# Moving modulation vectors from the attention stage into the first down projection, and splitting activations once

## The chip, the cores and the metric

The kernel runs on one core of a Trainium2 chip. The metric is the device time of one execution in microseconds; a time is the median of several runs.

## The reference

One transformer-like block on 512 tokens of width 1024, batch 1, all in float32. A condition vector c gives nine modulation vectors of 1024 numbers: shift, scale and gate of each of three sublayers.

```python
c_act = silu(c)
ada = c_act @ w_ada + b_ada          # w_ada: 1024 x 9216
sh1, sc1, g1, sh2, sc2, g2, sh3, sc3, g3 = split(ada, 9)
h = rmsnorm(x, ffn1_norm) * (1 + sc1) + sh1
x = x + 0.5 * g1 * (silu(h @ wg) * (h @ wu)) @ w_out1      # 1024 -> 2816 -> 1024
h = rmsnorm(x, mix_norm) * (1 + sc2) + sh2
z = h @ w_in        # latents, chunk q, k, v, two branch gates
y_a = latent_attention(z) @ w_branch_a
y_b = chunk_attention(z, rel_bias) @ w_branch_b
x = x + g2 * ((sigmoid(gA) * y_a + sigmoid(gB) * y_b) @ w_out)
h = rmsnorm(x, ffn2_norm) * (1 + sc3) + sh3
x = x + 0.5 * g3 * (silu(h @ wg2) * (h @ wu2)) @ w_out2
return rmsnorm(x, final_norm)
```

## The kernel before

**Number format.** Each float32 operand of a matmul is split into a high part (a cast by ACT, `L199`) and a low part (source minus high part, by DVE or POOL, `L200`). A product is three matmuls: high by high, low by high, high by low (`mm3`, L212; its three lines L215, L216 and L217 are the names by which the profile shows them).

**Stages** in order of time, in us of the profiled execution: a first piece of the up projection with the first two modulation vectors (0 to 55), the rest of the first up projection (to 252, `up_plain` and `up_fast`), the first `down` (252 to 378), the attention stage called the mixer (to about 700), a `down` with w_out (to 756), the second up projection (to 995) and the second `down` (to 1120).

**`down` (L637).** Two halves of 512 output columns. A half runs over 11 steps u; a step loads a 512 KB weight tile (`raw<-w2a`), splits it (`wh`, `wl`), splits the activations of two blocks of 128 features (`act_h`, `act_l`, `act_parts` at L632) and does 24 matmuls of 512 columns into four PSUM banks, one per block of 128 tokens. Half 1 holds back its last three steps and does them token block by token block, so that the update of x (L669, L670), the norm and the transposes (L253) of a block can begin while the next block is multiplied.

**Modulation vectors** (`vectors`, L345) are a generator. Vectors are numbered 0 to 8 (shift, scale and gate of the three sublayers). One step of it is one 512 KB load of w_ada and one DVE instruction: for shift and scale a row dot product (`ada_dot`, L301), for a gate a multiply-add into a row (`ada_step`, L297). After the eighth step of a gate its row is split and summed over partitions by four matmuls with a matrix of ones (`ada_rows`, L320; L327 and L328), and ACT writes it out (L329). Before the change vector 2 runs in `up_fast`; 4 and 3 in the first `down`, one step per u (16 loads); 7, 6 and 5 in the mixer, one step each time the helper `Fill` begins a projection (its `side`, L142), and what is left after the attention; 8 in the second `down`.

**The mixer** alternates heads of attention (`Head`, L67) with projections that `Fill` (L122) puts between. A head computes scores (L215 to L217 or L990, L991 on PE), a mask and row minimum (L83 on DVE), an exponential (L85 on ACT), a reciprocal and a scaling (L86, L87 on DVE), transposes (L95 on PE), a split of these (L98 on ACT, L99 on DVE) and the product with the values (L109 on PE). Weights are split by ACT and POOL there.

**Order and buffers.** PE's order is the order of the code. The order of the other engines is set by the framework's scheduler, which works from its own estimate of when inputs are ready. Every weight of these stages passes through one ring `raw` of 4 tiles of 512 KB, loaded in order by SP (`raw`, L192); the split weights through a ring `wh`/`wl` of 3 pairs; activations and other things through 22 tiles of one size (`slot`). ACT's own queue loads x again for the first `down` (L1053).

Of the kernel before, what the change touches and what calls it, by code (L numbers as in the profile page):

```python
# [10 lines left out]
F32 = mybir.dt.float32  # L11
F32R = mybir.dt.float32r
# [6 lines left out]
P = 128  # L19
S = 512  # L20
D = 1024
# [3 lines left out]
NF = FF // P  # L25
# [15 lines left out]
LAG_DOWN, LAG_OUT = 2, 0  # L41
EARLY_UP, FLUSH_UP = 3, (0, 2)
F1, F2 = 2, 2
WEIGHTS_A = ("raw",) * 4 + ("ada",)
WEIGHTS_B = ("raw",) * 4 + ("gate",) * 2 + ("ada",)
FLUSH_LAT = {0: 2, 1: 1}
# [20 lines left out]
class Head:  # L67
    def __init__(self, blk, h, scores, mask, v, out):
        self.blk, self.nc, self.h, self.scores_into, self.mask, self.out = blk, blk.nc, h, scores, mask, out
        self.probs = blk.sc4((P, 10 * P))  # L70
        self.st = blk.stat()
        self.v = v
        self.offs = [P * (qi * (qi + 1) // 2) for qi in range(NT)]
        self.pts = {}
# [45 lines left out]


class Fill:  # L122
    def __init__(self, ahead, side):
        self.jobs, self.ready, self.run, self.ahead, self.side = [], [], None, ahead, side

    def add(self, prepare, run):
        self.jobs.append((prepare, run))
# [6 lines left out]
    def __call__(self, n):  # L134
        while n > 0:
            if self.run is None:
                self.look(1)
                if not self.ready:
                    return
                run, units = self.ready.pop(0)  # L140
                self.run = run(units)
                self.side()  # L142
                self.look(self.ahead)
            try:
                next(self.run)
                n -= 1
            except StopIteration:
                self.run = None
# [5 lines left out]
class Block:  # L154
# [149 lines left out]
    def ada_columns(self, vec):  # L304
        io, nc = self.io, self.nc
        layer, kind = divmod(vec, 3)
        res = self.ring.tile([P, KT], F32, tag="adac", name="adac", bufs=2) if kind else self.shift[layer]
        for m in range(KT):
            self.ada_dot(self.raw(D, io["w_ada"][vec, m]), vec, m, res[:, m:m + 1])
            yield m == KT - 1  # L310
        if kind:
            col = (COL_FFN1, COL_MIX, COL_FFN2)[layer]
            nc.vector.scalar_tensor_tensor(
                self.scale[layer], res, 1.0, self.cols[:, col:col + KT], op0=ALU.add, op1=ALU.mult)
        yield True
# [1 line left out]
    def gate_row(self, name="gate_bc"):  # L317
        return self.fix.tile([P, D], F32, tag="gate", name=name, bufs=2)

    def ada_rows(self, acc):  # L320
        nc = self.nc
        hi, lo = (self.ring.tile([P, D], F32R, tag="w" + p, name="gate_" + p) for p in "hl")
        self.split(acc, hi, lo)
        for hf in range(2):
            cs = slice(hf * 512, (hf + 1) * 512)
            ps = self.bank(self.ada_bank)
            nc.tensor.matmul(ps, self.ones, hi[:, cs], start=True, stop=False)  # L327
            nc.tensor.matmul(ps, self.ones, lo[:, cs], start=False, stop=True)  # L328
            nc.scalar.mul(acc[:, cs], ps, 0.5)  # L329

    def ada_gate(self, vec):
        io, nc = self.io, self.nc
        layer = vec // 3
        if layer not in self.gate:
            self.gate[layer] = self.gate_row()
        acc = self.gate[layer]
        nc.gpsimd.memset(acc, 0.0)
        nc.scalar.dma_start(acc[0:1], io["b_ada"][:, vec * D:(vec + 1) * D])
        for j in range(KT):
            self.ada_step(acc, j, self.raw(D, io["w_ada"][vec, j]))  # L340
            yield j == KT - 1
        self.ada_rows(acc)
        yield True

    def vectors(self, vecs):  # L345
# [284 lines left out]
                side(n)  # L630

    def act_parts(self, u):  # L632
        pair = [self.slot([P, 2, S], F32R, "act_" + p) for p in "hl"]
        self.split(self.acts[u], *pair)
        return [[z[:, j] for z in pair] for j in range(2)]

    def down(self, parts, nk, w2, layer, tail, after, lag=0, store=None, side=None):  # L637
        nc = self.nc
        nu = nk // 2
# [256 lines left out]

    def mix(self, after):
        nc = self.nc
        gen = self.vectors((7, 6, 5))
        self.fill = Fill(2, lambda: self.advance(gen, 1))  # L900
        merged = self.attention()
        for _ in range(3):
            self.advance(gen, 99)
        self.low_engine = nc.vector
        self.x = self.fix.tile([P, NT, D], F32, tag="x16", name="x_back")
        for t in range(NT):
            nc.scalar.dma_start(self.x[:, t], self.x_home[t])

        parts = lambda u: [[merged[2 * u + j][:, i] for i in range(2)] for j in range(2)]
        self.down(parts, KT, self.io["w_out"], 1, KT // 2, after, LAG_OUT, store=self.slot)  # L910
# [130 lines left out]

    def layer(self, banks):
        nc, io = self.nc, self.io
        self.acts = []
        for f in range(F0):
            self.swiglu(f, banks[2 * f], banks[2 * f + 1])
        self.rope_angles()
        self.up_plain(io["w1a"], range(F0, F0 + F1), {0: self.mix_all})
        gen = self.vectors((2,))
        self.up_fast(io["w1a"], range(F0 + F1, NF), WEIGHTS_A, lambda n: self.advance(gen, n > 4))  # L1050
        self.x = self.fix.tile([P, NT, D], F32, tag="x16", name="x_again")
        for t in range(NT):
            nc.scalar.dma_start(self.x[:, t], io["x"][t * P:(t + 1) * P])  # L1053
        late = self.vectors((4, 3))
        self.down(self.act_parts, NF, io["w2a"], 0, 3, lambda t, xn: self.norm_token(t, 1, xn), LAG_DOWN,
                  side=lambda hf, u: self.advance(late, 1))
        self.mix(lambda t, xn: self.norm_token(t, 2, xn))

        def finish(t, o32):
            z = self.slot([P, D], F32, "out")  # L1060
            nc.gpsimd.tensor_tensor(z[:, :512], self.x[:, t, :512], fin[:, :512], op=ALU.mult)
            nc.vector.tensor_tensor(z[:, 512:], self.x[:, t, 512:], fin[:, 512:], op=ALU.mult)
            nc.scalar.mul(z[:, :512], z[:, :512], self.rstd[:, t:t + 1])
            nc.sync.dma_start(io["out"][t * P:(t + 1) * P, :512], z[:, :512])
            nc.vector.tensor_scalar(z[:, 512:], z[:, 512:], self.rstd[:, t:t + 1], None, op0=ALU.mult)
            nc.scalar.dma_start(io["out"][t * P:(t + 1) * P, 512:], z[:, 512:])
        gen = self.vectors((8,))
        self.acts = []
        for t in range(NT):
            nc.scalar.dma_start(self.x_home[t], self.x[:, t])  # L1070
        mixes = {EARLY_UP + j - 1: lambda j=j: self.mix_tokens(j) for j in range(2)}
        self.up_plain(io["w1b"], range(F2), mixes, EARLY_UP, FLUSH_UP)
        self.up_fast(io["w1b"], range(F2, NF), WEIGHTS_B)
        fin = self.gate_row("final_gain")
        nc.scalar.dma_start(fin, io["final"].to_broadcast([P, D]))
        self.x = self.fix.tile([P, NT, D], F32, tag="x16", name="x_last")
        for t in range(NT):
            nc.scalar.dma_start(self.x[:, t], self.x_home[t])
        self.ada_bank = "mm"

        def side(hf, u):
            if not hf:
                self.advance(gen, 1 if u < 9 else 99)
        self.down(self.act_parts, NF, io["w2b"], 2, 3, finish, side=side)
# [79 lines left out]
```

## Time and profile before

| what | us |
|---|---|
| median of 3 runs (lowest, highest) | 1136.0 (1134.95, 1137.53) |
| the profiled execution's own time | 1129.48 |
| its span in the trace | 1127.7 |
| PE busy in the span | 1074.9 |
| DVE busy in the span | 806.4 |
| ACT busy in the span | 589.4 |
| POOL busy in the span | 140.1 |

The span is what the trace shows from the first to the last instruction; the own time is that of the same execution. PE = TensorE matmul, PEld = its weight load, DVE = VectorE, ACT = ScalarE, POOL = GpSimd, SP = SyncE, which here only issues loads. A row of the timeline gives start, duration, engine, line, operation, the tiles written and read, and in brackets the idle time before it and what ended that. Tiles of one name are many buffers.

### The profile page before, as it was taken

To read this page: it belongs to the slowest core of one execution; us is meant where nothing else is said; L and a number is where in the kernel's file an instruction comes from. 1 tells how busy PE (TensorE), PEld (TensorE's weight loads), DVE (VectorE), ACT (ScalarE), POOL (GpSimd) and SP (SyncE) were. 2 spreads that over 40 slices of the span, in tenths; PEclk is the share of its full clock that TensorE was granted. 3 is DMA by queue.
4 is the path that set the end of the run, shared out by engine and by line. 5 is a ranking of instruction groups with operands and counts; after the bars stand their busy time and mean duration, and the time that the engine had idled before them with its cause. 6 is when DMAs were issued, how large, how long until landed. Compare 5 with 4: busy or idle time off the path is not lost.

```text
span 1127.7 us, 16891 instructions
## 1 busy us (share of the span) xinstructions
PE 1074.9 (95%) x6496; PEld 944.1 (84%) x6496; DVE 806.4 (72%) x1297; ACT 589.4 (52%) x1086; POOL 140.1 (12%) x126
## 2 busy tenths in 40 slices
PE   4999999999999999999889799999999999999997
PEld 3789999988887879877777678888999999988885
DVE  5898899877774767776877831458978788676724
ACT  5545555654443757655556533337555555654512
POOL 1000000000000112333443335200000000000200
PEclk9999999999999999999999999999999999999999
DMA  9723445257554422323443322442333333274322
GB/s 361 254 94 107 139 156 163 94 203 222 170 170 146 162 80 76 131 94 112 127 130 127 122 91 79 151 166 94 114 107 99 112 113 112 77 256 136 108 61 75
DMA packets 43575, 152.04 MB, mean 135 GB/s; under 512 B 5219, under 2 KB 5219, under 8 KB 43494
## 3 DMA queue, kind: packets, MB, share of 16 engines
q1 hardware_dynamic: 38160, 136.20, 36.6%
q10 hardware_dynamic: 5334, 14.76, 3.5%
q8 instruction: 51, 0.84, 0.3%
q14 instruction: 30, 0.25, 0.1%
HBM read 144.65 MB, written 6.29 MB: 134 GB/s over the span
## 4 chain that ended last, share of the span: by engine, by line
PE 76%; DVE 9%; DMA 5%; ACT 5%; issue 2%; POOL 2%; ACTq 0%; POOLq 0%; DVEq 0%
PE ps_mm L215 7%; PE ps_mm L216 7%; PE ps_mm L217 7%; PE ps_s L578 5%; PE ps_s L576 5%; PE ps_s L577 5%; DMA raw<-w_ada 3%; PE ps_t L578 3%; PE ps_t L577 3%; PE ps_t L576 3%; PE ps_s L216 2%; PE ps_s L217 2%; PE ps_s L215 2%; PE ps_t L215 2%; PE ps_t L216 2%
## 5 line engine op out<-in xcount | busy, mean ns | idle before, releaser
L199 ACT CAST wh<-raw 128x1024 fp32r<-128x1024 f32 x148 | 155.1, 1051 | 158.3 <-PE ps_o L217 47.7
L200 DVE TENSOR_TENSOR wl<-raw,wh 128x1024 fp32r<-128x1024 f32 x116 | 142.4, 1230 | 67.6 <-ACT wh L199 67.4
L215 PE MATMUL ps_mm<-h_hi,wh 128*128 128x512 f32 (+1 forms) x264 | 103.3, 391 | 0.0
L217 PE MATMUL ps_mm<-h_hi,wl 128*128 128x512 f32 (+1 forms) x264 | 100.5, 381 | 1.9 <-DVE wl L200 1.9
L216 PE MATMUL ps_mm<-h_lo,wh 128*128 128x512 f32 (+1 forms) x264 | 100.5, 381 | 0.2 <-DVE h_lo L200 0.2
L200 POOL TENSOR_TENSOR wl<-raw,wh 128x1024 fp32r<-128x1024 f32 x32 | 77.6, 2428 | 84.9 <-ACT wh L199 84.8
L578 PE MATMUL ps_s<-sum_h,wl 128*128 128x256 f32 x296 | 82.8, 280 | 0.0
L578 PE MATMUL ps_t<-sum_h,wl 128*128 128x256 f32 x296 | 82.7, 279 | 0.0
L577 PE MATMUL ps_t<-sum_l,wh 128*128 128x256 f32 x296 | 82.7, 279 | 0.0
L576 PE MATMUL ps_t<-sum_h,wh 128*128 128x256 f32 x296 | 82.6, 279 | 0.0
L577 PE MATMUL ps_s<-sum_l,wh 128*128 128x256 f32 x296 | 82.6, 279 | 0.0
L576 PE MATMUL ps_s<-sum_h,wh 128*128 128x256 f32 x296 | 82.6, 279 | 0.0
L200 DVE TENSOR_TENSOR act_l<-act,act_h 128x1024 fp32r<-128x1024 f32 x44 | 53.2, 1221 | 23.8 <-PE ps_t L216 20.2
L222 POOL TENSOR_TENSOR rstd<-ss,neghalf 128x1 f32<-128x1 f32 x16 | 10.4, 648 | 468.2 <-DVE ss L232 459.3
L217 PEld LDWEIGHTS ps_mm<-h_hi,wl 128*128 128x128 f32 x264 | 50.7, 192 | 12.3 <-DVE wl L200 2.1
L85 ACT ACTIVATE sc<-sc,stat 128x128 f32<-128x128 f32 (+1 forms) x64 | 35.9, 561 | 45.9 <-DVE stat L83 45.5
L216 PEld LDWEIGHTS ps_mm<-h_lo,wh 128*128 128x128 f32 x264 | 50.9, 193 | 7.5 <-DVE h_lo L200 0.4
L215 PEld LDWEIGHTS ps_mm<-h_hi,wh 128*128 128x128 f32 x264 | 51.0, 193 | 7.1
L578 PEld LDWEIGHTS ps_s<-sum_h,wl 128*128 128x128 f32 x296 | 55.6, 188 | 0.1
L301 DVE CUSTOM_DVE_ANT_0 raw<-raw,c_row,cols_sb 128x1024 f32<-128x1024 f32 x32 | 41.0, 1281 | 20.6 <-DMA raw<-w_ada 18.3
L576 PEld LDWEIGHTS ps_t<-sum_h,wh 128*128 128x128 f32 x296 | 55.7, 188 | 0.0
L577 PEld LDWEIGHTS ps_t<-sum_l,wh 128*128 128x128 f32 x296 | 55.6, 188 | 0.0
(380 smaller groups left out, 3289.2 us busy)
## 6 DMA issues: line engine op xcount, KB each, us to landing
raw<-w_ada SPq DMA_DIRECT2D x56, 512.0 KB, 3.6
raw<-w1a SPq DMA_DIRECT2D x32, 512.0 KB, 3.5
raw<-w1b SPq DMA_DIRECT2D x28, 512.0 KB, 3.5
raw<-w2a SPq DMA_DIRECT2D x22, 512.0 KB, 3.7
raw<-w2b SPq DMA_DIRECT2D x22, 512.0 KB, 3.7
w_first<-w_first SPq DMA_DIRECT2D x16, 512.0 KB, 9.6
raw<-w_gate SPq DMA_DIRECT2D x16, 512.0 KB, 3.5
raw_g<-w1b SPq DMA_DIRECT2D x11, 512.0 KB, 3.6
```

The costliest lines, as they stand in the source:

```text
L85: nc.scalar.activation(p, p, AF.Exp, scale=-1.0, bias=low, accum_out=tot)
L199: nc.scalar.copy(hi, src)
L200: (low_engine or nc.vector).tensor_tensor(lo, src, hi.bitcast(F32), op=ALU.subtract)
L215: mm(ps, lh, rh, start=start, stop=False)
L216: mm(ps, lh, rl, start=False, stop=False)
L217: mm(ps, ll, rh, start=False, stop=stop)
L222: nc.gpsimd.tensor_tensor(out, mean, self.neghalf[:, :n], op=ALU.pow)
L301: self.nc.vector.tensor_tensor_reduce(w, w, self.c_row, 1.0, self.cols[:, b:b + 1], ALU.mult, ALU.add, out)
L576: mm(ps, hi[:, cs], lh, start=start and k == 0, stop=False, skip_group_check=not start)
L577: mm(ps, hi[:, cs], ll, start=False, stop=False, skip_group_check=not start)
L578: mm(ps, lo[:, cs], lh, start=False, stop=k == 3, skip_group_check=not start)
```

## The change

Vectors 7, 6 and 5 (24 loads, 16 dots and 8 multiply-adds, and the four matmuls of gate 5) go from the mixer into the first `down`. There two steps per u run for the vectors 4, 3, 7, 6 and 5 (only one half-1 step, u = 10, has none), and the three steps that are left, the last of which makes the gate's row, stand behind `down`. `Fill` loses its `side`. The gate is summed up in another tile (`ada_acc`, in the place "ada"), and its row is allocated when it is made.

Activations are split once instead of in each half: `act_parts` keeps the pairs of u = 3 to 6 in the tiles hH and hL (the normed tokens, whose last reader is `up_fast`), those of u = 1, 2 and 7 to 10 in slots, and puts u = 0's pair of half 0 into the `wh`/`wl` ring; u = 0 alone is split again in half 1. That holds for both large `down` stages. Lines from L632 on stand 12 to 15 lower in the changed kernel.

```diff
@@ class Fill
-    def __init__(self, ahead, side):
-        self.jobs, self.ready, self.run, self.ahead, self.side = [], [], None, ahead, side
+    def __init__(self, ahead):
+        self.jobs, self.ready, self.run, self.ahead = [], [], None, ahead
...
                 self.run = run(units)
-                self.side()
                 self.look(self.ahead)
@@ class Block
-    def ada_rows(self, acc):
+    def ada_rows(self, acc, out):
...
-            nc.scalar.mul(acc[:, cs], ps, 0.5)
+            nc.scalar.mul(out[:, cs], ps, 0.5)
 
     def ada_gate(self, vec):
         io, nc = self.io, self.nc
         layer = vec // 3
-        if layer not in self.gate:
-            self.gate[layer] = self.gate_row()
-        acc = self.gate[layer]
+        acc = self.gate[layer] if layer in self.gate else self.main.tile([P, D], F32, tag="ada", name="ada_acc", bufs=1)
...
-        self.ada_rows(acc)
+        if layer not in self.gate:
+            self.gate[layer] = self.gate_row()
+        self.ada_rows(acc, self.gate[layer])
         yield True
...
     def act_parts(self, u):
-        pair = [self.slot([P, 2, S], F32R, "act_" + p) for p in "hl"]
-        self.split(self.acts[u], *pair)
+        if u not in self.act_pairs:
+            if not u and u not in self.act_seen:
+                pair = [self.ring.tile([P, 2, S], F32R, tag="w" + p, name="act_" + p) for p in "hl"]
+            else:
+                if u in ACT_IN_H:
+                    o = 2 * (u - ACT_IN_H[0])
+                    pair = [z[:, o:o + 2] for z in (self.hH, self.hL)]
+                else:
+                    pair = [self.slot([P, 2, S], F32R, "act_" + p) for p in "hl"]
+                self.act_pairs[u] = pair
+            self.split(self.acts[u], *pair)
+            self.act_seen.append(u)
+        else:
+            pair = self.act_pairs[u]
         return [[z[:, j] for z in pair] for j in range(2)]
...
     def mix(self, after):
         nc = self.nc
-        gen = self.vectors((7, 6, 5))
-        self.fill = Fill(2, lambda: self.advance(gen, 1))
+        self.fill = Fill(2)
         merged = self.attention()
-        for _ in range(3):
-            self.advance(gen, 99)
...
-        late = self.vectors((4, 3))
-        self.down(self.act_parts, NF, io["w2a"], 0, 3, lambda t, xn: self.norm_token(t, 1, xn), LAG_DOWN,
-                  side=lambda hf, u: self.advance(late, 1))
+        late = self.vectors((4, 3, 7, 6, 5))
+
+        def vector_steps(hf, u):
+            for _ in range(2):
+                if hf < 1 or u < 10:
+                    self.advance(late, 1)
+        self.down(self.act_parts, NF, io["w2a"], 0, 3, lambda t, xn: self.norm_token(t, 1, xn), LAG_DOWN, side=vector_steps)
+        for _ in range(8):
+            self.advance(late, 1)
         self.mix(lambda t, xn: self.norm_token(t, 2, xn))
```

**Where instructions move: the start of the first `down`, DVE.** L621 and L628 end the last step of `up_fast`. The row L301 that reads raw_2838 is the fourth dot of the late vectors in the changed kernel; raw_2760, wh_2762 and wl_2763 are the weight of u = 0. Before:

```order
L301 ISA raw_2869,adac_2794<-raw_2869,c_row_99,cols_sb_78 128x1024
L301 ISA adac_2794 128x1
L619 TENSOR_TENSOR sc4_2656<-ps_t_2653,sc4_2656 128x256
L621 TENSOR_TENSOR sc4_2656<-ps_s_2652,sc4_2656 128x256
L628 TENSOR_TENSOR act_2628<-sc4_2656,sc4_2747 128x2x2x128
L200 TENSOR_TENSOR wl_2763<-raw_2760,wh_2762 128x1024
L200 TENSOR_TENSOR wl_2801<-raw_2798,wh_2800 128x1024
```

In the changed kernel a dot more stands between L619 and L621, another between L628 and the low part of the first weight, and the low part of u = 0's activations, which stood further ahead, stands behind that:

```order
L619 TENSOR_TENSOR sc4_2656<-ps_t_2653,sc4_2656 128x256
L301 ISA raw_2838,adac_2794<-raw_2838,c_row_99,cols_sb_78 128x1024
L301 ISA adac_2794 128x1
L621 TENSOR_TENSOR sc4_2656<-ps_s_2652,sc4_2656 128x256
L628 TENSOR_TENSOR act_2628<-sc4_2656,sc4_2747 128x2x2x128
L301 ISA raw_2875,adac_2794<-raw_2875,c_row_99,cols_sb_78 128x1024
L301 ISA adac_2794 128x1
L200 TENSOR_TENSOR wl_2763<-raw_2760,wh_2762 128x1024
L200 TENSOR_TENSOR act_l_2767<-act_461,act_h_2766 128x1024
L200 TENSOR_TENSOR wl_2804<-raw_2801,wh_2803 128x1024
```

**SP at the same place.** The loads of the changed kernel, of which raw_2875 is the eighth from u = 0's weight on:

```order
L194 DMA raw_2760<-w2a 128x1024
L194 DMA raw_2795<-w_ada 128x1024
L194 DMA raw_2798<-w_ada 128x1024
L194 DMA raw_2801<-w2a 128x1024
L194 DMA raw_2835<-w_ada 128x1024
L194 DMA raw_2838<-w_ada 128x1024
L194 DMA raw_2841<-w2a 128x1024
L194 DMA raw_2875<-w_ada 128x1024
L194 DMA raw_2878<-w_ada 128x1024
L194 DMA raw_2881<-w2a 128x1024
```

Before, loads of w2a and of w_ada took turns one by one; now two of w_ada follow each of w2a.

**The end of the first `down`, PE.** In the changed kernel the four matmuls of gate 5 stand between the last matmul of `down` (L217, ps_o) and the first of the mixer (L215, wlat):

```order
L216 MATMUL ps_o<-wl,act_h 128x512
L217 MATMUL ps_o<-wh,act_l 128x512
L327 MATMUL ps_t<-gate_h,ones 128x512
L328 MATMUL ps_t<-gate_l,ones 128x512
L327 MATMUL ps_t<-gate_h,ones 128x512
L328 MATMUL ps_t<-gate_l,ones 128x512
L215 MATMUL ps_s<-wlat,h_hi 128x416
```

On DVE, gate_l stands behind the update of x for the last token block (there L681 and L682, which were L669 and L670):

```order
L681 TENSOR_TENSOR sc_3669<-ps_o,gate_bc 128x512
L200 TENSOR_TENSOR h_lo<-sc_3573,h_hi 128x4x128
L682 TENSOR_TENSOR x_again<-x_again,sc_3669 128x512
L200 TENSOR_TENSOR gate_l<-ada_acc,gate_h 128x1024
```

Before, these four matmuls and this split stood between two projections in the mixer.

## Rows read from the trace of the kernel before

**Rows 1.** Windows, first down and mixer: busy (count) of PE, PEld, DVE, ACT, POOL; PEclk, DMA share, GB/s.
```profile
252.00:374.00 122.00, 121.24 (x522) 97.10 (x523) 83.31 (x103) 52.21 (x67) 1.09 (x2) 1.00 0.59 189
400.00:655.00 255.00, 231.59 (x1245) 193.72 (x1244) 188.95 (x474) 148.24 (x355) 84.65 (x77) 0.97 0.33 108
```

**Rows 2.** Costliest groups by form, DVE, 400 to 655: busy, mean ns | idle before, releaser.
```profile
L301 DVE CUSTOM_DVE_ANT_0 raw<-raw,c_row,cols_sb 128x1024 f32<-128x1024 f32 x14 | 17.9, 1281 | 14.0 <-DMA raw<-w_ada 11.8 <-issue 2.0
L297 DVE SCALAR_TENSOR_TENSOR gate_bc<-raw,cact,gate_bc 128x1024 f32<-128x1024 f32 x8 | 12.4, 1556 | 6.4 <-DMA raw<-w_ada 6.2
```

**Rows 3.** Waits of PE, 400 to 655: total us, times, longest.
```profile
PE ps_o L109 <- DVE pt L99: 9.1, 9, 2.4
PE ps_t L95 <- DVE sc L87: 6.7, 3, 2.9
PE ps_s L990 <- DVE stat L83: 3.9, 3, 2.1
```

**Rows 4.** The same waits of PE, 400 to 500.
```profile
PE ps_o L109 <- DVE pt L99: 3.7, 5, 1.8
```

**Rows 5.** Timeline of the mixer at two vector steps, DVE and PE.
```profile
517.87 1.28 DVE L301 CUSTOM_DVE_ANT_0 raw<-raw,c_row,cols_sb 128x1024 f32<-128x1024 f32 x1 [3.19 <-DMA raw<-w_ada]
...
520.54 0.33 PE L95 MATMUL ps_t<-ident,sc 128*128 128x128 f32 x1 [2.08 <-DVE sc L87]
...
583.73 3.46 DVE L297 SCALAR_TENSOR_TENSOR gate_bc<-raw,cact,gate_bc 128x1024 f32<-128x1024 f32 x1 [2.37 <-DMA raw<-w_ada]
...
587.64 0.38 PE L109 MATMUL ps_o<-pt,vs 128*128 128x256 f32 x1 [2.43 <-DVE pt L99]
```

**Rows 6.** Timeline of the mixer at a weight split on POOL.
```profile
466.27 4.73 POOL L200 TENSOR_TENSOR wl<-raw,wh 128x1024 fp32r<-128x1024 f32 x2 [4.56 <-ACT wh L199]
...
468.61 2.61 DVE L87 TENSOR_SCALAR sc<-sc,stat 128x384 f32<-128x384 f32 x1
```

**Rows 7.** Windows of the mixer at a lower granted clock.
```profile
521.90:525.30 3.40, 3.40 (x12) 2.92 (x11) 2.40 (x10) 2.16 (x7) 2.13 (x1) 0.50 0.24 52
590.20:593.60 3.40, 3.40 (x10) 2.65 (x9) 2.27 (x3) 0.59 (x2) 0.63 (x2) 0.51 0.66 263
644.80:651.60 6.80, 6.01 (x18) 4.87 (x17) 3.86 (x14) 2.68 (x9) 0.00 (x0) 0.50 0.22 78
```

**Rows 8.** Timeline, 672 to 680: gate 5's row.
```profile
675.58 1.23 DVE L200 TENSOR_TENSOR gate_l<-gate_bc,gate_h 128x1024 fp32r<-128x1024 f32 x1 [0.90 <-ACT gate_h L199]
675.60 0.50 PE L327 MATMUL ps_t<-gate_h,ones 128*128 128x512 f32 x1 [0.95 <-ACT gate_h L199]
676.86 0.50 PE L328 MATMUL ps_t<-gate_l,ones 128*128 128x512 f32 x1 [0.76 <-DVE gate_l L200]
```

**Rows 9.** Timeline at the start of the first down.
```profile
247.75 1.28 DVE L301 CUSTOM_DVE_ANT_0 raw<-raw,c_row,cols_sb 128x1024 f32<-128x1024 f32 x1 [0.96 <-DMA raw<-w_ada]
...
249.07 0.33 SPq L194 DMA_DIRECT2D raw<-w2a  x1
...
253.46 0.40 PE L217 MATMUL ps_s<-wh,act_l 128*128 128x512 f32 x1
```

**Rows 10.** Tile raw, 240 to 262: its DMA.
```profile
DMA to landing us min/median/max: 3.6/4.4/7.0
```

**Rows 11.** Window at the start of the first down.
```profile
249.00:254.00 5.00, 2.84 (x18) 2.18 (x17) 3.55 (x7) 3.89 (x6) 0.00 (x0) 1.00 0.90 346
```

**Rows 12.** Costliest groups, 252 to 374: ACT's cast of weights.
```profile
L199 ACT CAST wh<-raw 128x1024 fp32r<-128x1024 f32 x21 | 22.0, 1052 | 39.9 <-PE ps_t L217 23.3 <-PE ps_o L217 16.6
```

**Rows 13.** Timeline at the end of the first down.
```profile
378.72 0.35 PE L215 MATMUL ps_s<-wlat,h_hi 128*128 128x416 f32 x1
...
380.63 0.69 DVE L670 TENSOR_TENSOR x_again<-x_again,sc 128x512 f32<-128x512 f32 x1
```

**Rows 14.** Timeline at the start of the second down.
```profile
994.97 0.38 ACT L625 ACTIVATE sc<-ps_o 128x256 f32<-128x256 f32 x1
...
996.50 0.40 PE L217 MATMUL ps_s<-wh,act_l 128*128 128x512 f32 x1
```

More of the change, by code (lines that the diff above doesn't have):

```diff
@@ L43 @@
 F1, F2 = 2, 2
+ACT_IN_H = range(3, 7)
 WEIGHTS_A = ("raw",) * 4 + ("ada",)
@@ L1043, in layer @@
         nc, io = self.nc, self.io
-        self.acts = []
+        self.acts, self.act_pairs, self.act_seen = [], {}, []
         for f in range(F0):
@@ L1067, in layer @@
         gen = self.vectors((8,))
-        self.acts = []
+        self.acts, self.act_pairs, self.act_seen = [], {}, []
         for t in range(NT):
```

## The prediction

> **What bounds the kernel now.** I read the windows first. In the first down PE is busy 121.24 of 122 us, with DVE at 83.31 and the transfers at 0.59 of the DMA engines' time; in the mixer's 255 us PE is busy 231.59, so 23.4 us idle, and its clock averages 0.97 [rows 1]. So the down stages are bound by PE with DVE to spare, and the mixer is where PE waits. The costliest groups show what the vector steps take there: 14 dots of 1.28 us and 8 multiply-adds of 1.56 us, 30.3 us of DVE, and DVE stands still another 18.0 us before them because the load of w_ada has not landed [rows 2]. DVE takes its instructions in order, so whatever stands behind such a step waits as well. PE's waits show who that is: 9.1 + 6.7 + 3.9 = 19.7 us in 15 waits on DVE's attention work [rows 3]. The timeline joins the two. A dot that waited 3.19 us for its load ends at 519.15, and PE gets its transpose's input 2.08 us late; a multiply-add that waited 2.37 us and took 3.46 costs PE 2.43 us [rows 5]. Not every wait is of this kind: before 500 PE waits five times, 3.7 us in all and 1.8 at most [rows 4], and ahead of the longest a scaling on DVE, with no vector step near it, takes 2.61 us beside splits on POOL [rows 6].
>
> **What leaves the mixer.** The five waits before 500 [rows 4] are short or beside POOL's splits and stay. The others, 19.7 - 3.7 = 16.0 us, stand behind vector steps; I take them as gone. After such waits PE's clock is granted at 0.50, the lower level of 1.2 GHz, for 3.4 us at 521.9, as long at 590.2, and 6.8 us at 644.8 [rows 7]: 13.6 us at half speed, which cost 6.8; I take 5.8 back, as a wait that stays may still bring one. Gate 5's row leaves with its two waits, 0.95 + 0.76 [rows 8]: 1.7. Together **-23.5**. Bounds: -12, if half of the waits only pass to the next late thing (POOL's splits, ACT's casts) and half of the slow clock stays; -30, if all 23.4 us of idle time and all 6.8 go.
>
> **What arrives at the start of the first down.** The order on DVE puts the fifth dot ahead of the low part of the first weight, without which PE cannot do its second matmul. Its load is the eighth from u = 0's weight on; SP issues it when the fourth dot frees a tile. In before the third dot ran at 247.75 and the load behind it left at 249.07 [rows 9]; the changed kernel has one more dot by then, so I put this load at 249.5. There ACT's queue is loading x again, and the DMA engines are busy 0.90 of the time at 346 GB/s [rows 11]. Landing takes 3.6 to 7.0 us, 4.4 in the middle [rows 10]. With 7.0: landed 256.5, dot 1.28, low part of the weight 1.22, low part of the activation 1.22 (it used to be early, now it stands behind; the price is that of a split of this size, 1.23 in [rows 8]), third matmul at 260.2 instead of 253.46 [rows 9], +6.8; with the median 4.4 +4.2. I take **+6**, nearer to the upper end because two more 512 KB loads are in flight there than before; bounds +2 (the load is issued and lands as early as any) and +9 (it waits behind a load of x). A wait of this length is like those before [rows 7], so 3.4 us at half speed may follow: **+1.7**, between 0 and 3.4.
>
> The Trainium skill, "DMA: Bandwidth & Descriptors", section "Specifications", gives about 358 GB/s as what one core gets from memory. By it the 346 of [rows 11] would leave almost nothing for a further load, and the seven-microsecond landing would be the rule at this place, 6.8 instead of 6 in the sum.
>
> **What arrives in the first down.** Three loads of 0.52 MB per u instead of two: at 5.58 us per u (24 matmuls, 522 of them in 121.24 us) 282 GB/s against 189. DVE gets 24 steps of about 1.3 us, 31 us, and loses 10 low parts of 1.22, so 83 becomes about 102 of 122 us; ACT loses 10 casts. None of that is on PE's path as long as loads keep up: ACT's cast of weights waited 39.9 us for PE to free a ring tile [rows 12], so weights run ahead. Nor do the removed splits gain anything here, since PE had no idle time there; the same holds for half 1 of the second down. The ring has four tiles: if c is the time from a load's issue to the end of its use, three loads per u need 3c/4 ≤ 5.58, c ≤ 7.4. With the median landing 4.4, a dot and a split ahead of it c is 6.9. I take **+1.5** for the places where it is tight, bounds 0 and the rival below.
>
> **What arrives at its end.** Gate 5's matmuls stand between the last matmul of down and the mixer's first, 378.72 [rows 13], and need gate_l, which stands on DVE behind the update of the last token block (380.63 + 0.69). It ends at 381.3 + 1.23 = 382.5, so PE waits 3.8 us where it had work (latents of earlier blocks). The work is done later and its own waits shrink by about 1 (a token block's norm has meanwhile become ready); with 0.9 for the matmuls, which leave the mixer too, nothing more: **+3.7** with the other waits of the new place taken at 0.9, bounds +1.5 and +6.
>
> **The second down.** u = 0's pair now comes through the ring behind the weight. Behind L625 at 994.97 + 0.38 [rows 14] come on ACT the casts of weight and activation, 2.1 us, on DVE the two low parts, 1.22 each: 995.35 + 1.05 + 1.22 + 1.22 = 998.8 plus small gaps, third matmul at 999.0 instead of 996.50 [rows 14]: **+2.5**, bounds +1 and +4. ACT's casts into hH stand ahead of copies that up_fast's last products need, one cast of 1.05 us in each of two stages; I take **+1** in all, bounds 0 and +2.
>
> **Sum.** -23.5 + 6 + 1.7 + 1.5 + 3.7 + 2.5 + 1 = -7.1 us. The profiled span of 1127.7 would be 1120.6, its own time 1129.48 would be 1122.4. The median of the runs lies 6.5 above that own time; I apply the difference to the median: 1136.0 - 7.1, about **1129**.
>
> **Rivals.** *The four-tile ring binds the first down (slower).* Place: DVE's dots in the first down, each waiting for its load, with weight splits in line behind them. Price: 3c/4 - 5.58 for each of 21 steps, less some 8 us by which weights run ahead at first (an estimate: one and a half steps, as the `wh`/`wl` ring has three pairs and one of them is in use). It turns the sum to no gain at c = 8.5 (0.80 x 21 - 8 = 8.7, in place of 1.5); at c = 9 the loss is 16.6 and the time 1136.0 - 7.1 + 15.1 = 1144. For it: the 7.0 landing at 249, plus a dot, is already 8.3 [rows 10], and DVE's dots stand among weight splits that wait for PE. Against: 7.0 was seen beside ACT's four loads of x only, and the DMA engines were busy 0.59 of the time [rows 1]; half as much again is 0.88. By the figure of the Trainium skill named above, 282 GB/s also stays under the limit and this rival falls; no run so far shows the stage at that rate.
>
> *The mixer gives back only half.* Waits on DVE pass to POOL, whose splits stretch DVE's work [rows 6], and half of the slow clock stays: -14 in place of -23.5, with the costs a little lower, 14: no change, 1136.
>
> *Start cheap, mixer complete.* The fifth load lands as the fastest did, 3.6 us, no slow clock follows, the end of the down costs 2, and the mixer gives 29: -29 + 3.4 + 2 + 2.5 + 1 = -20, 1116.
>
> *The change does not do what it says.* The order on the engines shows the loads, dots and matmuls at their new places, so I give it nothing.
>
> **How the numbers follow.** The forecast (1124 to 1133) gets 0.50, half a gain 0.18, the ring 0.17, the cheap start 0.15. A measurement of this kernel tells a change from none at about 0.2%, 2.3 us. Faster: the forecast nearly whole (0.48), the cheap start (0.15): 0.63. Same: most of the half gain and a little of the others, 0.15. Slower: the ring and the rest, 0.22. The range reaches from the cheap start, 1116, to a ring with c a little under 9, 1143.
>
> **What would show it.** Right: between 400 and 700 no row L301 or L297 is left, PE's waits on L99, L87 and L83 fall from 19.7 to about 4, and no window there shows the clock at 0.50; at about 258 to 260 the first L217 of the first down; PE waits 3 to 4 us for L328 near the end of that stage. Wrong: PE idle by more than 3 us in the first down after its first step (the ring), ACT's wait for PE there gone from 39.9 to near nothing, or the mixer still with 10 us of waits on DVE.

## The result, and the profile after

| | before | after |
|---|---|---|
| median (lowest, highest), us | 1135.47 (1132.48, 1137.53), 4 runs | 1120.18 (1118.98, 1121.90), 4 runs |
| profiled span, us | 1127.7 | 1117.1 |

The ratio is 0.9868, interval [0.9842, 0.9895]: faster by 15.3 us. The prediction was 7 us less than before; the time lies inside its range, but not in the 1124 to 1133 to which it gave half its chances. The profiled spans differ by 10.6 us only; where the other 4.7 are is the matter of one of the runs.

The windows after, for the first down, the mixer, and two places of the first down:

```profile
252.00:374.00 122.00, 111.41 (x468) 89.15 (x468) 86.47 (x110) 33.84 (x40) 0.00 (x0) 0.96 0.76 251
400.00:655.00 255.00, 251.20 (x1401) 216.07 (x1401) 172.61 (x477) 167.85 (x408) 84.39 (x79) 1.00 0.22 71
254.00:264.00 10.00, 4.88 (x10) 3.20 (x11) 7.01 (x9) 5.58 (x6) 0.00 (x0) 0.50 0.61 214
376.00:380.00 4.00, 3.50 (x7) 2.44 (x8) 3.37 (x5) 1.79 (x3) 0.00 (x0) 0.50 0.87 284
```

Against [rows 1] the two stages have changed places: the mixer's idle time of PE fell from 23.4 to 3.8 us and its clock rose from 0.97 to 1.00, while in the window of the first down PE, which had lost 0.8 us, loses 10.6, and the stage has two stretches at 0.50. No row L301 or L297 is left in the mixer.

The waits of PE in the mixer after, which answer to [rows 3] (one line was added above them, so L99 is L100, and L95 is L96):

```profile
PE ps_o L110 <- DVE pt L100: 2.0, 2, 1.5
PE ps_t L977 <- DVE kT L954: 0.7, 1, 0.7
PE ps_s L1000 <- DVE ca_k L871: 0.6, 1, 0.6
PE ps_t L96 <- DVE qT L979: 0.4, 1, 0.4
```

Of 19.7 us two waits are left, 2.0 together; the longer, of 1.5, is the one beside POOL's splits that [rows 6] show (here the scaling took 2.31 us). The waits of PE in the first down, 252 to 400:

```profile
PE ps_mm L215 <- ACT wh L199: 5.5, 1, 5.5
PE ps_s L216 <- DVE wl L200: 4.8, 1, 4.8
PE ps_s L215 <- ACT act_h L199: 2.4, 1, 2.4
PE ps_t L327 <- ACT gate_h L199: 1.5, 1, 1.5
PE ps_t L328 <- DVE gate_l L200: 1.1, 1, 1.1
```

The second and third are the start, the last two gate 5's row; the first, the longest, stands in no step of the prediction. The timeline at the start:

```profile
250.13 8.51 SPq L194 DMA_DIRECT2D raw<-w_ada  x2
...
256.99 1.28 DVE L301 CUSTOM_DVE_ANT_0 raw<-raw,c_row,cols_sb 128x1024 f32<-128x1024 f32 x1 [4.24 <-DMA raw<-w_ada]
...
258.20 1.22 DVE L200 TENSOR_TENSOR wl<-raw,wh 128x1024 fp32r<-128x1024 f32 x1
...
260.61 0.80 PE L217 MATMUL ps_s<-wh,act_l 128*128 128x512 f32 x1 [0.34 <-DVE act_l L200]
```

The fifth dot's load left at 250.13 and landed 6.8 us later, DVE stood still 4.24 us, and the third matmul came at 260.61 (253.46 before, [rows 9]; 260.2 in the prediction's sum with a landing of 7.0). And ACT at the end of the same stage:

```profile
374.15 0.89 ACT L199 CAST wlat<-raw 128x832 fp32r<-128x832 f32 x1 [9.77 <-DMA raw<-w_lat]
374.94 1.04 ACT L199 CAST wh<-raw 128x1024 fp32r<-128x1024 f32 x1
```

A cast of w_lat, the mixer's first weight, stands on ACT ahead of the cast of down's last weight, and waits for a load that SP issued behind the last loads of w_ada. That order on ACT was there before the change too; only then w_lat landed in time.

To place the losses I read three starts in each trace's timeline: PE's first matmul of the first down (A), its first one of half 1 (B), and its first one with wlat, which begins the mixer (C):

| kernel | A | A to B | B to C |
|---|---|---|---|
| before | 251.87 | 62.72 | 64.13 |
| after | 253.95 | 69.07 | 75.97 |

Together with the mixer (C to the first matmul with merged, the tile of the attention's output: 343.70 before, 311.35 after) the trace of the change reads: start 2.1 + 6.4, end 11.8 (gate 5's row and its matmuls 4.6 of it), mixer -32.4, second down and the rest 1.5, sum -10.6.

### The profile page after: what moved, and what is told of

It is laid out like the page before. It is cut to its first block, busy times and chain, and to the rows that moved or that the text cites. A ratio compares the mean times of both kernels' runs of the same rounds, so it can differ in the third digit from the quotient of the medians.

```text
span 1117.1 us, 16843 instructions
## 1 busy us (share of the span) xinstructions
PE 1068.8 (96%) x6496; PEld 942.9 (84%) x6496; DVE 780.1 (70%) x1277; ACT 570.7 (51%) x1066; POOL 135.8 (12%) x126
## 4 chain that ended last, share of the span: by engine, by line
PE 76%; DVE 9%; DMA 8%; ACT 3%; issue 3%; ACTq 0%; POOL 0%; POOLq 0%; DVEq 0%
PE ps_mm L215 9%; PE ps_mm L216 9%; PE ps_mm L217 9%; DMA raw<-w_ada 7%; PE ps_s L578 4%; PE ps_s L576 4%; PE ps_s L577 4%; PE ps_t L577 3%; PE ps_t L578 3%; PE ps_t L576 3%; PE ps_s L217 2%; PE ps_s L216 2%; PE ps_s L215 2%; PE ps_o L576 2%; DVE w_first L301 2%
## 5 line engine op out<-in xcount | busy, mean ns | idle before, releaser
L215 PE MATMUL ps_mm<-h_hi,wh 128*128 128x512 f32 (+1 forms) x264 | 101.5, 384 | 0.0
L217 PE MATMUL ps_mm<-h_hi,wl 128*128 128x512 f32 (+1 forms) x264 | 98.9, 375 | 1.9 <-DVE wl L200 1.9
L217 PEld LDWEIGHTS ps_mm<-h_hi,wl 128*128 128x128 f32 x264 | 49.7, 188 | 12.0 <-DVE wl L200 2.1
L301 DVE CUSTOM_DVE_ANT_0 raw<-raw,c_row,cols_sb 128x1024 f32<-128x1024 f32 x32 | 41.0, 1284 | 24.9 <-DMA raw<-w_ada 24.7
L578 PEld LDWEIGHTS ps_t<-sum_h,wl 128*128 128x128 f32 x296 | 55.6, 188 | 0.6 <-DVE wl L200 0.6
L576 PEld LDWEIGHTS ps_s<-sum_h,wh 128*128 128x128 f32 x296 | 55.6, 188 | 0.1
L577 PEld LDWEIGHTS ps_s<-sum_l,wh 128*128 128x128 f32 x296 | 55.6, 188 | 0.0
L215 PEld LDWEIGHTS ps_mm<-h_hi,wh 128*128 128x128 f32 x264 | 49.8, 188 | 6.9
```

The costliest lines, as they stand in the source:

```text
L215: mm(ps, lh, rh, start=start, stop=False)
L217: mm(ps, ll, rh, start=False, stop=stop)
L301: self.nc.vector.tensor_tensor_reduce(w, w, self.c_row, 1.0, self.cols[:, b:b + 1], ALU.mult, ALU.add, out)
L576: mm(ps, hi[:, cs], lh, start=start and k == 0, stop=False, skip_group_check=not start)
L577: mm(ps, hi[:, cs], ll, start=False, stop=False, skip_group_check=not start)
L578: mm(ps, lo[:, cs], lh, start=False, stop=k == 3, skip_group_check=not start)
```

## The experiments

All ratios are to the kernel before on the same chip. The groups ran on different chips, where the medians of before lay between 1134.4 and 1136.8 us, so a difference of medians across groups is good to about 2 us.

**Only the vectors moved.** `act_parts` is that of the kernel before.

```diff
-        if u not in self.act_pairs:
...
+        pair = [self.slot([P, 2, S], F32R, "act_" + p) for p in "hl"]
+        self.split(self.acts[u], *pair)
```

> The vectors are moved as in the change, but the activations are split in each half as before. Theory A (the whole gain is the mixer without vector steps, about 32 us in the trace; what is lost is lost in the first down: at its start, where the fifth dot stands ahead of the first weight's low part, at its end, where the casts of w_lat stand on ACT ahead of the last weight's cast and their loads come late, and at gate 5's row): in this order only one dot stands ahead of the first low part, so the start is back to within 2 us of before, the end still costs about 10, the gate 4; 1112 to 1117. Theory B (part of the gain is the splitting once, which gives DVE and ACT room in the first down): slower than the change, 1123 to 1128.

1120.43 us, 0.9865 [0.9841, 0.9890]: the same as the change. So the splitting once neither pays nor costs in it. The expected cheap start was a miss (A to B is 69.58): the fifth dot still stands ahead of L627 (L628 before), which is ahead of the first low part, and that was enough. Its timeline:

```profile
256.58 1.28 DVE L300 CUSTOM_DVE_ANT_0 raw<-raw,c_row,cols_sb 128x1024 f32<-128x1024 f32 x1 [4.74 <-DMA raw<-w_ada]
...
257.79 0.69 DVE L627 TENSOR_TENSOR act<-sc,sc 128x512 f32<-128x512 f32 x1
258.40 3.49 DVE L199 TENSOR_TENSOR wl<-raw,wh 128x1024 fp32r<-128x1024 f32 x3
```

**Only the splitting.** The change's `act_parts` in the kernel before.

```diff
-        pair = [self.slot([P, 2, S], F32R, "act_" + p) for p in "hl"]
+        if u not in self.act_pairs:
...
```

> Activations are split once as in the change, the vectors stay in the mixer as before. Theory A: the removed splits gain nothing, u = 0's pair behind the first weight costs 2 to 3 us at the start of each down: 1136 to 1140. Theory B: faster than before by 4 to 8 us, 1127 to 1131.

1146.26 us, 1.0085 [1.0060, 1.0110]: slower by 11 us, more than either theory said. Only some 3 us of that are u = 0's pair behind the first weight (0.9 ahead of A, and the 1.9 that the second down costs in the change too); most of the rest is order, as the edit changes what the scheduler puts ahead of what. At the start of the second down a step of vector 8 came to stand ahead of the first low part:

```profile
1009.59 1.28 DVE L298 SCALAR_TENSOR_TENSOR gate_bc<-raw,cact,gate_bc 128x1024 f32<-128x1024 f32 x1 [2.97 <-DMA raw<-w_ada]
1010.79 1.22 DVE L201 TENSOR_TENSOR wl<-raw,wh 128x1024 fp32r<-128x1024 f32 x1
...
1012.07 0.80 PE L217 MATMUL ps_s<-wl,act_h 128*128 128x512 f32 x1 [3.74 <-DVE wl L201]
```

This is the wait that the change has at the first down; with it and its slow clock the second down's start cost 7.7 us here and 1.9 in the change. In `up_fast` a multiply-add of vector 2, which waited 2.50 us for its load, came to stand ahead of two low parts; PE waited 1.79 us there at 171.82, and some 3 us of the 11 were lost by the end of that stage.

**The price of the steps in the mixer.** The kernel before without vectors 7, 6 and 5.

```diff
-        gen = self.vectors((7, 6, 5))
-        self.fill = Fill(2, lambda: self.advance(gen, 1))
+        self.fill = Fill(2, lambda: None)
+        nc.gpsimd.memset(self.scale[2], 1.0)
+        nc.gpsimd.memset(self.shift[2], 0.0)
...
+        self.gate[1] = self.gate_row()
+        nc.gpsimd.memset(self.gate[1], 0.5)
```

> The kernel before without vectors 7, 6 and 5 (their 24 loads, dots and multiply-adds and gate 5's row are left out, constants in their place): the price of these steps in the mixer alone. Theory A: 32 us in the trace go and nothing is paid elsewhere; a median 32 to 37 under before, 1099 to 1104. Rival (the mixer's waits pass to POOL's splits and the change gains by something else): 12 to 20 under before, 1115 to 1123.

1099.34 us, 0.9683 [0.9658, 0.9707]: 35.8 us, as theory A expected. So the change gained 35.8 us in the mixer and paid 20.5 of it back elsewhere (15.3 left). The mixer is left bound by PE:

```profile
400.00:655.00 255.00, 249.86 (x1366) 211.56 (x1366) 166.11 (x441) 158.61 (x370) 93.70 (x83) 1.00 0.23 71
```

**Before once more.** No edit.

> The kernel before, unchanged, for a second profile. The median moved by 15.3 us, the two profiled spans by 10.6 only. Theory A: the runs of before vary by some microseconds in the mixer, where DVE's queue hangs on when loads of w_ada land, and its first profile was a short one; this profile's mixer (from the first transposes of q to the first matmul with merged) differs from the first one's by 2 to 6 us, the down stages by under 1. Rival: the difference lies in the first 55 us or is spread over all stages.

1135.53 us, 1.0003 [0.9985, 1.0021], with a span of 1134.4: 6.7 longer than that of the first profile. Of it 2.4 had come by C and 3.6 came in the mixer, where PE's largest wait (400 to 660) was longer than in [rows 3]:

```profile
PE ps_o L109 <- DVE pt L99: 10.1, 10, 2.5
```

The first profile of before, 1129.48, was its shortest run of all; the others in this study lay between 1130.05 and 1141.42 us. The expectation held for the mixer; the stages ahead of it moved by more than the 1 us that was expected. A to B was 64.27, with 3.4 us at 0.50 from 255 on, of which the first profile has none: so of the 6.4 us at the start above, 1.6 is no more than two profiles of before differ by.

**The start spared.** No steps at the first three u.

```diff
-            for _ in range(2):
+            for _ in range((0 if u < 3 else 2) if hf < 1 else 3 if u < 6 else 2):
                 if hf < 1 or u < 10:
```

> The change, but without vector steps at the first three u of half 0 of the first down; half 1 runs three steps at its first six u instead, and ends where the change ended. No dot stands ahead of the first weights' low parts any more. Theory A (the wait at the start is the fifth dot's load): the first product of the first down begins within 3 us of where it did before the change (253.5 for the third matmul) and there is no slow clock there; 7 to 10 us less than the change, 1110 to 1113, and 4 us less than that if the last weight's cast, which in this order has no cast of w_lat ahead of it, no longer holds PE. Rival C (the start is held by the loads of x and the weight's own load, which are late anyway): 1119 to 1121. The four-tile ring (rival of the prediction): PE waits in half 1, where four loads per u are asked for, by 3 us or more.

1115.69 us, 0.9826 [0.9793, 0.9860], 4.5 us less than the change and short of the 7 to 10 expected. A to B is 64.93: the dot's wait is gone. The slow clock is not, though it is shorter:

```profile
255.00:262.00 7.00, 6.46 (x17) 5.04 (x17) 6.55 (x9) 4.80 (x6) 0.00 (x0) 0.53 0.59 165
```

It makes up the 2.2 us that stay. With u = 0's pair behind the first weight PE waits 2.35 us for act_h ahead of A, which stays at 254.18 (1.41 before, for the weight), and 0.54 for act_l, and the products behind them run at 0.50. B to C is 74.26, as late as ever, though no cast of w_lat stands ahead of a weight's on ACT any more: here the last weight's low part waits on DVE behind multiply-adds that wait for their loads.

```profile
371.35 1.28 DVE L297 SCALAR_TENSOR_TENSOR ada_acc<-raw,cact,ada_acc 128x1024 f32<-128x1024 f32 x1 [0.52 <-DMA raw<-w_ada]
...
372.55 1.22 DVE L200 TENSOR_TENSOR wl<-raw,wh 128x1024 fp32r<-128x1024 f32 x1
```

So ACT's order is one form that the late end takes, not its only cause. PE waits 6.6 us in half 1, all after 366 and 4.9 of it for this low part; that is the sign that the expectation gave for the ring, and the fifth tile below asks whether it was.

**Vector 4 in up_fast.** The steps of the first down end at u = 6 of half 1.

```diff
-        gen = self.vectors((2,))
-        self.up_fast(io["w1a"], range(F0 + F1, NF), WEIGHTS_A, lambda n: self.advance(gen, n > 4))
+        gen = self.vectors((2, 4))
+        self.up_fast(io["w1a"], range(F0 + F1, NF), WEIGHTS_A, lambda n: self.advance(gen, 1))
+        self.advance(gen, 99)
...
-        late = self.vectors((4, 3, 7, 6, 5))
+        late = self.vectors((3, 7, 6, 5))
```

> The change, but vector 4 runs in up_fast behind vector 2, one step per f from the first on; the first down has only vectors 3, 7, 6 and 5, two steps per u from u = 0, which end at u = 6 of half 1 with gate 5's row. The start's order is that of the change. Theory A (the end of the first down loses because the loads of w_lat queue behind the last loads of w_ada, and because gate 5's row is needed at once): PE's wait for the last weight (5.7 us in the change), the slow clock after it and the waits for the row (3 us) go; the start keeps its 5 us wait; up_fast loses 0 to 3; 1108 to 1114. Rival D (the end is late by itself, whatever is queued): 1119 to 1122.

1115.77 us, 0.9824 [0.9784, 0.9865], 4.4 us less than the change and 1.8 over the most that was expected. B to C is 65.87: 10.1 of the 11.8 us are back, gate 5's row, now ahead of down's end, included. The rest of the trace, which is that of the longest of four runs, paid: A came 4.1 us later, and PE waited 7.2 us for the first low part, against 4.8 in the change. So the end was late because the last loads of w_ada ran into it.

**Both.** Vector 4 in up_fast as in the last diff, and three steps per u at u = 3 to 6 of half 0, then two.

```diff
-            for _ in range(2):
+            for _ in range((0 if u < 3 else 3 if u < 7 else 2) if hf < 1 else 2):
```

> Both of these: vector 4 in up_fast, and no steps at the first three u of the first down (three per u from u = 3 to 6, then two). Theory A: nearly all that the change lost in the first down comes back: 1100 to 1106. If start and end hide each other (PE waits at the end for what the start had delayed), no better than the better one of the two alone.

1109.91 us, 0.9777 [0.9740, 0.9815]: 10.3 us under the change, more than either repair alone (4.5 and 4.4), but short of the 14 to 20 expected. A to B is 64.93, with 6.8 us at 0.50 as when the start alone was spared; B to C is 67.05.

**Both, with the old splitting.** `act_parts` as before.

> The same with the activations split in each half as before. Theory A (splitting once gains nothing and puts u = 0's pair behind the first weight): 2 to 5 us faster than with the change's splitting, 1097 to 1102. Theory B (splitting once gives DVE and ACT room that the moved vectors need): slower by 3 us or more.

1108.09 us, 0.9768 [0.9726, 0.9810], 1.8 us less than the last one; the intervals overlap, so neither theory is borne out by the times. In the trace A to B is 62.73, that of the kernel before to 0.01. PE's wait for act_h ahead of A is gone and so is the slow clock behind it:

```profile
255.00:262.00 7.00, 7.00 (x32) 5.64 (x31) 7.00 (x8) 5.26 (x6) 0.00 (x0) 1.00 0.70 225
```

But B to C is 69.66, 2.6 more than with the pairs kept, for PE waits for the last weight again:

```profile
PE ps_mm L214 <- ACT wh L198: 2.7, 1, 2.7
```

Three casts of w_lat stand on ACT ahead of that weight's cast, and the third's load landed only at 362.9, though the last load of w_ada had left at 343.7.

**A fifth tile for loads**, on the change: every fifth load goes into the place "ada".

```diff
     def raw(self, n, src):
+        if self.five is not None and n == D:
+            self.five += 1
+            if self.five % 5 == 0:
+                t = self.main.tile([P, D], F32, tag="ada", name="raw_a", bufs=1)
+                self.nc.sync.dma_start(t, src)
+                return t
...
```

> The change with a fifth tile for loads in the first down, until vector 5 begins: every fifth 512 KB load goes into the place "ada", which is idle there. In the change the window 262 to 350 moved 251 to 267 GB/s where three loads per u want 282, so weights lose their lead. Theory E (the four-tile ring binds the first down, the prediction's rival, and the late end is its bill): the rate rises to 275 GB/s or more and PE's wait at the last weights (5.5 us in the change, with the slow clock after it) shrinks to 2 us or less; with what the fourth dot costs at the start about as in the change 1110 to 1114, less if one dot less stands ahead of the first weight. Theory F (the late end is only the order of loads and of ACT's queue around w_lat): the wait stays over 4 us, 1118 to 1121.

1121.08 us, 0.9864 [0.9842, 0.9886]: no gain. The rate did not rise to 275: from 262 to 350 it was 267, 262 and 236 GB/s in three windows, against 251, 254 and 267 in the change. The window 290 to 320 of the change:

```profile
290.00:320.00 30.00, 30.00 (x132) 24.29 (x131) 19.02 (x26) 6.15 (x6) 0.00 (x0) 1.00 0.78 254
```

and of this kernel:

```profile
290.00:320.00 30.00, 30.00 (x132) 24.35 (x131) 22.17 (x30) 5.59 (x6) 0.00 (x0) 1.00 0.81 262
```

Theory E falls as far as the number of tiles goes. The wait at the last weights did shrink, from 5.5 to 2.7, where theory E wanted 2 or less and theory F over 4, and the start's grew from 4.8 to 5.6.

**The steps ended earlier.** Vector 4 in up_fast, old splitting, three steps per u from u = 3 through half 0. Against the kernel with both repairs and the old splitting:

```diff
-            for _ in range((0 if u < 3 else 3 if u < 7 else 2) if hf < 1 else 2):
+            for _ in range((0 if u < 3 else 3) if hf < 1 else 2):
```

> Vector 4 in up_fast, no steps at the first three u, splitting as before, and now three steps per u through half 0 and two in half 1, so that the last step comes at u = 5 of half 1. Theory E: the ring gives no more than some 300 GB/s, the steps stretch over a longer time than asked for, and PE's wait near the end (2.7 us in the last run with two steps per u) changes by less than 1 us or grows: 1106 to 1110. Theory F (the end is a matter of when the last loads of w_ada stand ahead of w_lat): the wait and its slow clock go, 1103 to 1106.

1102.60 us, 0.9703 [0.9677, 0.9728]: 17.6 us under the change and 3.3 over the kernel that leaves the 24 steps out (19 and 2 by the ratios). The wait at the end and its slow clock are gone, as theory F expected; B to C is 66.37. Four loads per u were asked for, and four tiles carried 296 GB/s with PE not idle:

```profile
290.00:320.00 30.00, 30.00 (x130) 24.17 (x129) 28.63 (x41) 11.35 (x14) 0.00 (x0) 1.00 0.87 296
```

Its waits of PE from 245 to 420:

```profile
PE ps_mm L215 <- DVE wl L199: 0.8, 1, 0.8
PE ps_s L215 <- DVE wl L199: 0.8, 1, 0.8
PE ps_mm L214 <- ACT wh L198: 0.4, 1, 0.4
```

**The same with a fifth tile.** The edit of the fifth tile on top.

> That one with the fifth tile. Theory E: 2 to 4 us faster than with four tiles, 1103 to 1106, the best so far; rival: within 1 us of it.

1102.59 us, 0.9699 [0.9678, 0.9720]: within 0.1 us of four tiles, as the rival said.

**Loads one step ahead**, in the kernel before's mixer.

```diff
-            self.ada_dot(self.raw(D, io["w_ada"][vec, m]), vec, m, res[:, m:m + 1])
+            if m < KT - early:
+                held.append(self.raw(D, io["w_ada"][vec, m + early]))
+            self.ada_dot(held.pop(0), vec, m, res[:, m:m + 1])
...
```

> The kernel before, with each load of w_ada for vectors 7, 6 and 5 issued one step ahead of the step that reads it (the first of each vector excepted): the same DVE work in the mixer, fewer of its waits for loads. Theory G (DVE standing still before the steps, 18 us of the 48 they hold it, is a good part of the mixer's 36 us): faster than before by 8 to 18 us, 1118 to 1128, with DVE's idle time before L301 and L297 under 6 us. Theory H (the steps' own time on DVE in the middle of its attention work is the price, or the held tile of the ring costs the weights as much): within 5 us of before, 1131 to 1141.

1133.95 us, 0.9977 [0.9956, 0.9998]. Inconclusive: the edit did not do what it was for. DVE waited for these loads as long as in [rows 2], 15.1 + 4.8 us:

```profile
L301 DVE CUSTOM_DVE_ANT_0 raw<-raw,c_row,cols_sb 128x1024 f32<-128x1024 f32 x14 | 17.9, 1280 | 16.2 <-DMA raw<-w_ada 15.1 <-issue 1.1
L297 DVE SCALAR_TENSOR_TENSOR gate_bc<-raw,cact,gate_bc 128x1024 f32<-128x1024 f32 x8 | 10.2, 1279 | 4.8 <-DMA raw<-w_ada 4.8
```

**Steps made small.** Loads and waits stay in the mixer, the steps' work goes.

```diff
+        if vec in (6, 7):
+            self.nc.vector.tensor_scalar(out, w[:, 0:1], 1.0, None, op0=ALU.mult)
+            return
...
+            if vec == 5:
+                nc.vector.tensor_scalar(acc[:, j:j + 1], w[:, 0:1], 1.0, None, op0=ALU.mult)
```

> The kernel before with the dots and multiply-adds of vectors 7, 6 and 5 shrunk to an instruction that reads one column of the loaded tile (the vectors are not computed); the 24 loads, their order and the waits for them stay in the mixer, only the steps' own 30 us on DVE go. Theory G (DVE standing still for loads is a good part of the mixer's 36 us): 8 to 20 us slower than without any steps (1099.3), 1107 to 1119. Theory H (the steps' own time is the price): within 5 us of it, 1099 to 1104.

1117.86 us, 0.9859 [0.9823, 0.9894]: 18.5 us above the kernel without any steps (1099.34), so 17.3 of the 35.8 us go with the steps' work. Of the 18.5, gate 5's row, which stays here, has 3.2 in the trace (from the third o_hl to the fourth). The rest goes with the 24 loads: 11.3 in the mixer of the trace (C to merged is 326.95, and 312.40 without steps), which is that of the shortest of four runs, and at most 15 by the medians. PE waits there for DVE's attention work, and never for a weight:

```profile
PE ps_o L109 <- DVE pt L99: 8.4, 8, 2.0
PE ps_s L997 <- DVE stat L83: 2.4, 2, 1.2
```

These are 7.5 us more than in the kernel without steps, which has 2.0 and 1.3 of them. So DVE's standing still is the larger part of the 11.3; that none of it is the ring tiles which the loads hold is not shown. DVE's waits stand in its rows with 0.15 us of work each:

```profile
L301 DVE TENSOR_SCALAR shift<-raw 128x1 f32<-128x1 f32 x8 | 1.2, 153 | 11.4 <-DMA raw<-w_ada 11.3
L345 DVE TENSOR_SCALAR gate_bc<-raw 128x1 f32<-128x1 f32 x8 | 1.2, 151 | 11.2 <-DMA raw<-w_ada 11.1
L301 DVE TENSOR_SCALAR adac<-raw 128x1 f32<-128x1 f32 x6 | 0.9, 152 | 4.2 <-DMA raw<-w_ada 4.2
```

Work and waiting do not add up cleanly: DVE waited 26.6 us for these loads here and 18.0 in [rows 2], so with less work to do it stood still for longer.

## Why the prediction was right in its sign and wrong in its size

**The mixer, -23.5: the step that failed.** Its mechanism held and its size did not: the trace gave -32.4 and the runs -35.8, beyond the bound of -30. From the eighth head's transposes of q to the third o_hl the working was right: the 16.0 us of waits and all 6.8 of the slow clock went, 23.0 us by the two traces. Three things were missed. First, "the five waits before 500 are short or beside POOL's splits and stay": only the longest did (1.77, now 1.5). The others, and stalls of under 1 us that are in no row of the prediction, went with the steps: from the first head's transposes of q to the eighth's the change is ahead of before by 5.0 us, and the kernel without steps by 5.1. Second, gate 5's row gave back 3.2 us and not 1.7, as its four matmuls leave the mixer too, and 1.2 that the prediction took off at the end of the first down came between C and the first head. Third, the sum was drawn from one profile, and that was the shortest run of before: its own time lay 6.5 us under the median, and the prediction carried the 6.5 over to the changed kernel, where it is 1.2.

**The start, +6 and +1.7: right, the second with luck.** The dot's load landed after 6.8 us, the third matmul came 7.2 us late, and the later A and the longer A to B are 8.4 together, against 7.7 and a part of the +1 for up_fast. But the clock was at 0.50 for 10 us, three times the 3.4 assumed; it cost no more because PE stood still for half of them. Nor was it the dot's alone: with the start spared, 6.8 us at 0.50 were left. The Trainium skill, "DMA: Bandwidth & Descriptors", section "Specifications", has about 358 GB/s for a core, by which the prediction had 6.8 us for this place. The trace agrees with the 6.8, as the third matmul came 7.2 us late, but not with the limit: beside the loads of x it moved 367 GB/s, and the measurement decides.

```profile
249.00:254.00 5.00, 2.65 (x24) 2.44 (x22) 2.13 (x4) 2.92 (x6) 0.00 (x0) 1.00 0.94 367
```

**The first down, +1.5: the second step that failed.** It measured 7.3 (11.84 less the row's 4.57). The prediction looked for the ring's loss in PE waiting step by step, found none and was right about that: from the first steps to 370 PE did not wait. But it did not ask what is queued behind the late loads of w_ada: on SP the loads of w_lat, and on ACT, behind a cast of w_lat, the cast of down's own last weight. Of the rival with the ring the lost lead came true (251, 254 and 267 GB/s from 262 to 350, where three loads per u want 282) but not its reason, as the fifth tile showed. What held the loads to that rate is open. Of the signs of being wrong, PE idle by more than 3 us after the first step came (5.5), but ACT's wait for PE did not fall from 39.9; it rose to 64.4, so the weights ran ahead until near the end:

```profile
L199 ACT CAST wh<-raw 128x1024 fp32r<-128x1024 f32 x21 | 21.9, 1050 | 70.2 <-PE ps_t L217 36.0 <-PE ps_o L217 20.6 <-PE ps_t L216 7.8
```

**Gate 5's row, +3.7:** 4.6 in the trace, near in size but made up otherwise: PE waited 1.5 us for gate_h and 1.1 for gate_l where 3.8 were expected for gate_l alone, and the four matmuls took 1.9, as the clock fell again at 397. **The second down, +2.5:** 1.9, right. **The removed splits:** priced at nothing, and the change is indeed the same without them; that the same edit alone costs 11 us no theory foresaw, and most of that is steps that the scheduler put elsewhere in DVE's queue.

Seen as a sum, the errors partly cancelled: gains of 35.8 instead of 23.5, costs of 20.5 instead of 16.4. In the trace alone the change is worth -10.6, against -7.1.

## What to carry to other kernels

A filler instruction that waits for its own load holds everything behind it in its engine's queue: here 24 such steps and their gate row cost 35.8 us in a stage that hung on DVE, 11 to 15 of them by waiting, and 2 to 3 in stages bound by PE, once they began after the first steps there and ended before the last loads. So move such work into a stage with slack, but look in the order of every queue for what stands right behind the first and the last of it. And before a stage is priced from one profile, compare that profile's time with the spread of the runs.

## What was not expected of the hardware

Four tiles of 512 KB, each loaded only when its last reader is done, carried 296 GB/s for 30 us, and with a fifth tile the time was the same (1102.60 and 1102.59 us).

The same waits need not bring the same clock: at the start of the first down both profiles of before have PE waiting 1.4 and 0.8 us, and one ran on at full clock while the other had 3.4 us at 0.50, the lower of the two levels.

Runs of one kernel differ by more than some of the effects above: before between 1133.25 and 1141.42 us in one group of 13 runs, the kernel with small steps between 1114.8 and 1121.4, the one with both repairs and the old splitting, which has no steps in the mixer, between 1106.6 and 1113.7, and the fastest one with four tiles between 1101.6 and 1104.0. What sets this spread is open.
